# Two transformer blocks on one core: when the adaLN products run, and which engine computes silu and the convolution's first tap

## The chip, the cores and the metric

The kernel runs on one core of one Trainium2 chip. The metric is the device time of one execution in microseconds (us), as the median of several runs. Five engines work in parallel, each on a queue of its own that it takes strictly in order: TensorE (PE, matmuls, with PEld for its weight loads), VectorE (DVE), ScalarE (ACT), GpSimd (POOL) and SyncE (SP, which issues most of the transfers here). An instruction starts when the one before it on its engine is done with and the semaphores that it waits for have come.

## What is computed

Two blocks of a transformer on 256 tokens with 1024 channels, in fp32. The first has an in-projection, a mixer of three branches (a gated linear recurrence "LRU", gated linear attention "GLA", and block attention "MoBA"), an out-projection and a SwiGLU FFN, with RMS norms. The second is a two-layer model whose norms are modulated by a condition vector c (adaLN): a short convolution with its FFN, then attention with forget gates ("FoX") with its FFN. Cut to what matters here:

```python
f = (silu(h @ w_ffn_gate) * (h @ w_ffn_up)) @ w_ffn_down      # all three FFNs have this form

shift, scale, gate, ... = split(silu(c) @ w_ada + b_ada)      # adaLN, and the same with w_ada_kv
h = x * (1 + scale) + shift

gb, gc, v = split(h @ w_in, 3)                                # short convolution
u = gc * v
y = (gb * (w0 * u[t-2] + w1 * u[t-1] + w2 * u[t])) @ w_out

k, v = h @ w_k, h @ w_v
log_f = log_sigmoid(h @ w_f + b_f)                            # forget gates
F = cumsum(log_f)
logits[t, s] = q[t] . k[s] / sqrt(d) + F[t] - F[s]            # s <= t
```

## The kernel before

Activations lie transposed, channels on the 128 partitions and the 256 tokens along the free axis, so 1024 channels are 8 tiles of 128x256. All weights come as 128x128 blocks in the order of use, eight to a tile `raw` of 128x1024 fp32 (512 KB, four buffers, issued by SP, L125). `weights` splits each tile: ACT rounds it to `wh` (L142), DVE subtracts to `wl` = raw − wh (L148), each with five buffers. A block's product is three matmuls, `wh` with the rounded activation, `wl` with it, and `wh` with the activation's rest (L160 to L162 in `mm3`, L195 to L201 in `ksteps`). Over the kernel there are 296 such tiles.

The adaLN products silu(c) @ w_ada are not matmuls. They are 112 calls of `gemv` (L360 on): SP loads a 512 KB tile `gw` (L366, three buffers), and DVE multiplies it by the broadcast silu(c), `cact`, and accumulates into one column of `ada` (L369). Where they stand in the program is set by a rate: each single product of a stage adds `grate` to an account, each pair twice that, and `fill` calls `gemv` whenever the account reaches one. `GR` holds the rates, for the first FFN, its down-projection with the norm, the convolution, the second block's first half (out-projection `co`, FFN), its down-projection, the keys, values and attention, and the last FFN. `ada_cols` (L387) makes all products that its columns still lack. `silu_c` (L470) loads c and computes `cact`.

The stages run in the order: in-projection and mixer; the out-projection of the first block (`partial("out")`, one k step per finished head pair, and `post_rms`); FFN 0; its down-projection `d0` with a norm; the convolution (first eight products in one `kouter`, then one by one; c_c L1200 on ACT, c_up L1203 and c_y L1205 to L1208 on DVE, then the split yh, yl); its out-projection `co` with a norm; FFN 1, whose first products are begun before the norm is known (`lazy`, finished by lz_c, ff_g, ff_u L1042 to L1049); `d1`; wk, wv and the forget gates (`fox_gates`, L813 to L835, with the logarithm and exponential at L825 and L826); FoX attention (fG enters the logits at L766); wo; FFN 2; `d2`.

A scheduler of the framework sets the order of each engine's queue from the program's order and its own simulated timeline. `after`, `pipeline` and `unbroken` pin some pairs (a gw behind the wl tile issued last, `self.anchor`). The silu of the FFNs is two instructions, `silu2` (L508): tanh(x/2) on ACT (L511, `silu_t`) and (t + 1) x on DVE (L513, `silu_o`), which is twice the silu. The factor 0.5 is put into the next product: in `ffn` either the row R2h, half of the norm's row R2, scales `ff_u` (L898), or the instruction of `ff_m` has it (L905).

Of the kernel before, what the change touches and what calls it, by code (L numbers as in the profile page):

```python
# [17 lines left out]
P = 128  # L18
D = 1024
T = 256  # L20
# [8 lines left out]
LN_EPS = 1e-5  # L29
GR = (0.55, 1.2, 0.35, 0.8, 1.0, 0.8, 0.3)  # L30
QF = 1
# [32 lines left out]
class Net:  # L64
# [443 lines left out]
    def silu2(self, src):  # L508
# [5 lines left out]
        return o  # L514

    def lru(self, xin, gin, R):
        nc = self.nc
# [368 lines left out]

    def ffn(self, l, X, R=None, R2=None, first=(), rows=None):

# [4 lines left out]
        def evac(g, u):  # L893
            if R is not None:
                g2 = self.tmp("ff_g")
                V.tensor_tensor(g2, g, R, ALU.mult)
                u2 = self.tmp("ff_u")
                V.tensor_tensor(u2, u, R2, ALU.mult)  # L898
                s = self.silu2(g2)
                m = self.tmp("ff_m")  # L900
                V.tensor_tensor(m, s, u2, ALU.mult)
            else:
                s = self.silu2(g)
                m = self.tmp("ff_m")
                V.scalar_tensor_tensor(m, s, 0.5, u, op0=ALU.mult, op1=ALU.mult)  # L905
            h = self.tl(self.fp, [P, T + 2], "mh", F32R)[:, 0:T]
# [158 lines left out]
    def run(self):  # L1065
# [34 lines left out]
        go = self.pair("in_go", 0, "in_go", 1, X)  # L1100
        mix[2], mix[3] = self.gla(qk, go, la, gv, R, rc)
        mvp = self.tokmajor("in_mv", 0, 4, X)
        mv = [[], []]
# [11 lines left out]
        for i in range(4):  # L1115
# [6 lines left out]
            V.tensor_tensor(k, ps[:, 1, :], R, ALU.mult)  # L1122
            Ls = [self.attn_p(q, k, hh, self.moba_head_bias(2 * i + hh)) for hh in range(2)]
            if i:
                step(Y, i - 1)
# [5 lines left out]
        for k in range(5, NK):  # L1131
            step(Y, k)
        X = Y
        self.close()


        fg, rp, head = self.post_rms("out", X, NK, "post_mix_norm", pre)
        x1, X, steps = [], ([], []), []
# [21 lines left out]
        A.activation(R, rp, AF.Copy)  # L1160
        Rh = self.tl(self.fp, [P, T], "R2h", bufs=1)
        A.activation(Rh, rp, AF.Copy, scale=0.5)
        self.silu_c()
        self.grate = GR[0]
        self.strict = STRICT[1]
        M = self.ffn(0, X, R, Rh)
        self.grate = GR[1]
# [27 lines left out]
        for i in range(NK):  # L1195
# [8 lines left out]
            y = self.tmp("c_y")  # L1204
            V.tensor_scalar(y, up[:, 0:T], self.vec("conv_w_2", i), None, ALU.mult)  # L1205
            for j in range(1, 3):
# [256 lines left out]
```

## Time and profile before

| | us |
|---|---|
| median of three runs | 1003.15 |
| lowest and highest | 1002.32, 1003.19 |
| the profiled execution | 1002.28 |
| its span in the trace | 1000.5 |
| mean granted TensorE clock | 0.973 of full speed |
| PE busy | 936.8 (94%) |
| DVE busy | 805.7 (81%) |
| ACT busy | 528.7 (53%) |

The span is what the trace covers, from the first instruction to the last. Busy time is what instructions took, waits left out. Matmuls overlap each other, so a single one reads longer in a list (0.28 us) than the distance between two; how many fit in a window tells PE's pace. The view of PE's waits lists which instruction PE waited for, by tile and line. Lists by line give the mean duration of one instruction in ns. Timelines give start and duration, and in brackets how long the engine had been idle before and what released it.

### The profile page before, as it was taken

Reading aid. Unit: us, or ns where it says so; the run is one execution under the profiler, and the core shown is the slowest. Engines: PE = TensorE matmul, PEld = TensorE weight load, DVE = VectorE, ACT = ScalarE, POOL = GpSimd, SP = SyncE. Lnnn points to the kernel's source line nnn. Section 1 sums busy time; section 2 is a strip of 40 time slices with the busy share of each in tenths; the row PEclk is TensorE's granted clock in tenths of the full one; section 3 lists DMA queues with packets and bytes.
Section 4 is the critical chain, followed back from the end, with each engine's and each line's share of the span. In section 5 each row is a group of like instructions: output and inputs, shape, how many; then the busy total and the mean of one; then the engine's idle time right before and its main releaser. Section 6 shows DMA issues by size and latency. Waiting matters only on the chain.

```text
span 1000.5 us, 19149 instructions
## 1 busy us (share of the span) xinstructions
PE 936.8 (94%) x7442; PEld 902.4 (90%) x7442; DVE 805.7 (81%) x1578; ACT 528.7 (53%) x941; POOL 20.2 (2%) x66
## 2 busy tenths in 40 slices
PE   7989988999999879999799999999899988999996
PEld 7879887999999879998699999997788888999995
DVE  8886578999997697779999989799665898866553
ACT  7574564445443444458354444487465675545431
POOL 1211000000000000000000000000000000000001
PEclk9999998999999999999899999999899999999998
DMA  8853237888899486744999989745542366556531
GB/s 304 269 174 104 85 112 269 278 294 283 285 361 379 145 296 205 230 148 151 309 302 337 342 322 340 276 149 182 197 148 64 107 206 218 187 189 190 184 112 43
DMA packets 62346, 219.56 MB, mean 219 GB/s; under 512 B 7112, under 2 KB 8784, under 8 KB 62256
## 3 DMA queue, kind: packets, MB, share of 16 engines
q1 hardware_dynamic: 61056, 215.06, 63.5%
q0 software_dynamic: 1056, 3.16, 1.1%
q8 instruction: 58, 0.95, 0.4%
q14 instruction: 32, 0.26, 0.1%
q10 hardware_dynamic: 144, 0.13, 0.0%
HBM read 217.26 MB, written 2.63 MB: 220 GB/s over the span
## 4 chain that ended last, share of the span: by engine, by line
PE 74%; DVE 16%; issue 3%; ACT 3%; DMA 3%; SPq 0%; DVEq 0%; ACTq 0%
PE acc L160 20%; PE acc L162 20%; PE acc L161 19%; DVE wl L148 5%; DMA raw<-wts 3%; PE acc L195 3%; PE acc L196 2%; PE acc L201 2%; DVE gw L369 1%; ACT wh L142 1%; DVE ln_w L1060 1%; PE ms L807 1%; DVE yl L265 1%; DVE fg L1057 1%; PE lg L760 1%
## 5 line engine op out<-in xcount | busy, mean ns | idle before, releaser
L148 DVE TENSOR_TENSOR wl<-raw,wh 128x1024 fp32r<-128x1024 f32 (+2 forms) x296 | 355.0, 1205 | 100.9 <-ACT wh L142 99.0
L142 ACT ACTIVATE wh<-raw 128x1024 fp32r<-128x1024 f32 (+2 forms) x296 | 308.0, 1047 | 240.4 <-PE acc L162 129.3
L160 PE MATMUL acc<-yh,wh 128*128 128x256 f32 x608 | 171.1, 282 | 3.4 <-DVE ff_m L905 3.4
L160 PE MATMUL acc<-xh,wh 128*128 128x256 f32 x576 | 165.6, 287 | 7.9 <-ACT c_c L1200 3.4
L162 PE MATMUL acc<-yl,wh 128*128 128x256 f32 x608 | 171.2, 282 | 0.0
L161 PE MATMUL acc<-yh,wl 128*128 128x256 f32 x608 | 170.6, 281 | 0.0
L162 PE MATMUL acc<-xl,wh 128*128 128x256 f32 x576 | 164.2, 285 | 0.0
L161 PE MATMUL acc<-xh,wl 128*128 128x256 f32 x576 | 164.1, 285 | 0.0
L161 PE MATMUL acc<-mh,wl 128*128 128x256 f32 x528 | 148.3, 281 | 0.0
L160 PE MATMUL acc<-mh,wh 128*128 128x256 f32 x528 | 148.3, 281 | 0.0
L162 PE MATMUL acc<-ml,wh 128*128 128x256 f32 x528 | 147.7, 281 | 0.0
L369 DVE SCALAR_TENSOR_TENSOR gw<-gw,cact 128x1024 f32<-128x1024 f32 x112 | 134.6, 1217 | 0.0
L160 PEld LDWEIGHTS acc<-xh,wh 128*128 128x128 f32 x576 | 111.5, 194 | 9.8 <-ACT c_c L1200 3.6
L160 PEld LDWEIGHTS acc<-yh,wh 128*128 128x128 f32 x608 | 115.2, 190 | 3.7 <-DVE ff_m L905 3.6
L161 PEld LDWEIGHTS acc<-yh,wl 128*128 128x128 f32 x608 | 115.3, 190 | 0.4 <-issue 0.4
L162 PEld LDWEIGHTS acc<-yl,wh 128*128 128x128 f32 x608 | 114.8, 189 | 0.6 <-issue 0.6
L161 PEld LDWEIGHTS acc<-xh,wl 128*128 128x128 f32 x576 | 111.7, 194 | 0.4 <-issue 0.3
L162 PEld LDWEIGHTS acc<-xl,wh 128*128 128x128 f32 x576 | 111.1, 193 | 0.0
L161 PEld LDWEIGHTS acc<-mh,wl 128*128 128x128 f32 x528 | 99.4, 188 | 0.0
L160 PEld LDWEIGHTS acc<-mh,wh 128*128 128x128 f32 x528 | 99.3, 188 | 0.0
L162 PEld LDWEIGHTS acc<-ml,wh 128*128 128x128 f32 x528 | 99.3, 189 | 0.0
L195 PE MATMUL acc<-xh,wh 128*128 128x256 f32 (+1 forms) x256 | 67.2, 293 | 9.1 <-ACT wh L142 5.6
(407 smaller groups left out, 1553.9 us busy)
## 6 DMA issues: line engine op xcount, KB each, us to landing
raw<-wts SPq DMA_DIRECT2D x288, 512.0 KB, 4.4
gw<-ada SPq DMA_DIRECT2D x112, 512.0 KB, 5.5
raw<-wts SPq DMA_DIRECT2D x6, 256.0 KB, 5.7
m_scr<-m_row POOLq DMA_DIRECT2D x2, 768.0 KB, 5.4
ax<-xT SPq DMA_DIRECT2D x4, 256.0 KB, 4.5
m_b<-m_scr POOLq DMA_DIRECT2D x8, 128.0 KB, 4.4
out<-fg SPq DMA_DIRECT2D x8, 128.0 KB, 1.8
cst<-cst SPq DMA_DIRECT2D x1, 588.5 KB, 7.1
```

Source lines behind the costliest of these rows:

```text
L142: i = nc.scalar.activation(self.wh[:, d], r, AF.Copy)
L148: self.anchor = nc.vector.tensor_tensor(self.wl[:, d], r, self.wh[:, d].bitcast(F32), ALU.subtract)
L160: m = [mm(ps, wh, xh, start=start, stop=False), mm(ps, wl, xh, start=False, stop=False), mm(ps, wh, xl, start=False, stop=stop)]
L161: mm(ps, wl, xh, start=False, stop=False),
L162: mm(ps, wh, xl, start=False, stop=stop)]
L195: m.append(mm(outs[i], wh, X[0][k], start=k == 0 and i % per == 0, stop=False))
L196: m.append(mm(outs[i], wl, X[0][k], start=False, stop=False))
L201: m.append(mm(outs[i], wh, X[1][k], start=False, stop=False))
L265: self.lo = self.nc.vector.tensor_tensor(l, src, h.bitcast(F32), ALU.subtract)
L369: i = nc.vector.scalar_tensor_tensor(t, t, 1.0, self.cact, op0=ALU.mult, op1=ALU.mult, accum_out=self.ada[:, g:g + 1])
L760: mm(lg[hh][:, o:o + w], q[r, t], k[r, 0:w], start=o == 0, stop=False)
L807: mm(pv[64 * hh:64 * hh + 64, o:T], v[tt][vo[hh] // T][:, vo[hh] % T:vo[hh] % T + 64], pts[hh][:, p], start=tt == 0, stop=tt == 1)
```

## The change

`GR` gets other rates (0 in the convolution, lower in the second block's first half, twice as high from the keys on), and `PRE` adds calls of `gemv` in the mixer: two for each head pair, one for each late step of the out-projection, and rate 2 in its norm. `silu_c` is called in the mixer. `silu` is one ACT instruction with the function Silu, so that `silu_o` and the factors 0.5 are left out, R2h with them. The convolution's first tap c_y is an ACT copy with a scale by partition.

```diff
--- before.py
+++ after.py
@@ -27,7 +27,8 @@
 ALPHA = 4.0 ** 0.25
 RMS_EPS = 1e-6
 LN_EPS = 1e-5
-GR = (0.55, 1.2, 0.35, 0.8, 1.0, 0.8, 0.3)
+GR = (0.6, 1.15, 0.0, 0.45, 1.1, 1.6, 0.25)
+PRE = (2, 1, 2)
 QF = 1
 EV = (4, 6, 3)
 LZ = (18, 27, 30)
@@ -512,6 +513,11 @@
         o = self.tmp("silu_o")
         self.nc.vector.scalar_tensor_tensor(o, t, 1.0, src, op0=ALU.add, op1=ALU.mult)
         return o
+
+    def silu(self, src):
+        t = self.tmp("silu_t")
+        self.nc.scalar.activation(t, src, AF.Silu)
+        return t
 
     def lru(self, xin, gin, R):
         nc = self.nc
@@ -884,7 +890,7 @@
         self.warm(WARM[1], rc[:, 0:1].broadcast_to([P, T]))
         return fg, rows, head
 
-    def ffn(self, l, X, R=None, R2=None, first=(), rows=None):
+    def ffn(self, l, X, R=None, first=(), rows=None):
 
         nc = self.nc
         V = nc.vector
@@ -895,14 +901,14 @@
                 g2 = self.tmp("ff_g")
                 V.tensor_tensor(g2, g, R, ALU.mult)
                 u2 = self.tmp("ff_u")
-                V.tensor_tensor(u2, u, R2, ALU.mult)
-                s = self.silu2(g2)
+                V.tensor_tensor(u2, u, R, ALU.mult)
+                s = self.silu(g2)
                 m = self.tmp("ff_m")
                 V.tensor_tensor(m, s, u2, ALU.mult)
             else:
-                s = self.silu2(g)
+                s = self.silu(g)
                 m = self.tmp("ff_m")
-                V.scalar_tensor_tensor(m, s, 0.5, u, op0=ALU.mult, op1=ALU.mult)
+                V.tensor_tensor(m, s, u, ALU.mult)
             h = self.tl(self.fp, [P, T + 2], "mh", F32R)[:, 0:T]
             lo = self.tl(self.fp, [P, T + 2], "ml", F32R)[:, 0:T]
             nc.scalar.activation(h, m, AF.Copy)
@@ -1099,6 +1105,7 @@
         gv = self.tokmajor("in_gv", 0, 2, X)
         go = self.pair("in_go", 0, "in_go", 1, X)
         mix[2], mix[3] = self.gla(qk, go, la, gv, R, rc)
+        self.silu_c()
         mvp = self.tokmajor("in_mv", 0, 4, X)
         mv = [[], []]
         for tt in range(2):
@@ -1121,6 +1128,7 @@
             k = self.tmp("a_k")
             V.tensor_tensor(k, ps[:, 1, :], R, ALU.mult)
             Ls = [self.attn_p(q, k, hh, self.moba_head_bias(2 * i + hh)) for hh in range(2)]
+            self.gemv(PRE[0])
             if i:
                 step(Y, i - 1)
                 head(i - 1, self.attn_out(i - 1, prev, mv))
@@ -1130,10 +1138,12 @@
         head(3, self.attn_out(3, prev, mv))
         for k in range(5, NK):
             step(Y, k)
+            self.gemv(PRE[1])
         X = Y
         self.close()
 
 
+        self.grate = PRE[2]
         fg, rp, head = self.post_rms("out", X, NK, "post_mix_norm", pre)
         x1, X, steps = [], ([], []), []
         sacc = self.tmp("sacc")
@@ -1158,12 +1168,9 @@
         self.fp = self.open("ffn0", NFF)
         R = self.tl(self.fp, [P, T], "R2", bufs=1)
         A.activation(R, rp, AF.Copy)
-        Rh = self.tl(self.fp, [P, T], "R2h", bufs=1)
-        A.activation(Rh, rp, AF.Copy, scale=0.5)
-        self.silu_c()
         self.grate = GR[0]
         self.strict = STRICT[1]
-        M = self.ffn(0, X, R, Rh)
+        M = self.ffn(0, X, R)
         self.grate = GR[1]
         fg, rp, head = self.post_rms("d0", M, NFF, "post_ffn_norm")
         self.close()
@@ -1202,7 +1209,7 @@
             G.memset(up[:, 0:2], 0.0)
             V.tensor_tensor(up[:, 2:], got[("ci_v", i)], c, ALU.mult)
             y = self.tmp("c_y")
-            V.tensor_scalar(y, up[:, 0:T], self.vec("conv_w_2", i), None, ALU.mult)
+            A.activation(y, up[:, 0:T], AF.Copy, scale=self.vec("conv_w_2", i))
             for j in range(1, 3):
                 V.scalar_tensor_tensor(y, up[:, j:j + T], self.vec("conv_w_2", 8 * j + i), y, op0=ALU.mult, op1=ALU.add)
             V.tensor_tensor(y, y, got[("ci_b", i)], ALU.mult)
```

The lines of the changed file stand one further up to the new function and six or seven further behind it: wl is L149, gw L370, a_q L1127, g_kc L655, c_up L1210, fG L839. The total of `gw` by stage, counted in the two orders of DVE: mixer with its out-projection 0, then 13; FFN 0 with 19, then 21; d0 23, 22; convolution 9, 0; FFN 1 30, 17; d1 17, 18; keys and values 1, 4; gates and attention 6, 11; FFN 2 7, 6. ACT has seven table loads before and ten in the change: one more for Silu in FFN 0 and one in FFN 2, and one that reloads the exponential's table at the forget gates.

DVE in the mixer, before, between the splits of two weight tiles and the first keys of GLA (l_ names are the LRU's, g_ and ls_ the GLA's, a_ the block attention's):

```order
L544 RECIPROCAL l_e_102_515<-l_e_102_515 128x256
L561 SCALAR_TENSOR_TENSOR l_e_107_533<-l_e_107_533,l_xc_521 128x256
L544 RECIPROCAL l_e_106_529<-l_e_106_529 128x256
L505 SCALAR_TENSOR_TENSOR g_z_474<-g_z_474,ls_l_483 128x258
L148 TENSOR_TENSOR wl_1058<-raw_1055,wh_1057 128x1024
L599 TENSOR_SCALAR nsp_93_489<-g_z_474 128x2
L600 TENSOR_SCALAR sp_94_490<-g_z_474 128x2
L602 TENSOR_SCALAR g_z_474<-g_z_474 128x256
L148 TENSOR_TENSOR wl_1128<-raw_1125,wh_1127 128x1024
L619 SCALAR_TENSOR_TENSOR g_cum_711<-resetm_166,g_z_474 128x256
L632 TENSOR_TENSOR ff_u_723<-g_cum_711 128x256
```

The same place in the change:

```order
L370 SCALAR_TENSOR_TENSOR gw_1137,ada_175<-gw_1137,cact_843 128x1024
L550 RECIPROCAL l_e_106_529<-l_e_106_529 128x256
L505 TENSOR_TENSOR ls_l_483<-ls_l_483,ls_a_477 128x258
L370 SCALAR_TENSOR_TENSOR gw_1140,ada_175<-gw_1140,cact_843 128x1024
L149 TENSOR_TENSOR wl_1146<-raw_1143,wh_1145 128x1024
L149 TENSOR_TENSOR wl_1198<-raw_1195,wh_1197 128x1024
L506 SCALAR_TENSOR_TENSOR g_z_474<-g_z_474,ls_l_483 128x258
L1127 SCALAR_TENSOR_TENSOR a_q_992<-acc_931,m_R_380 128x256
L1129 TENSOR_TENSOR a_k_994<-acc_931,m_R_380 128x256
L149 TENSOR_TENSOR wl_1228<-raw_1225,wh_1227 128x1024
L370 SCALAR_TENSOR_TENSOR gw_1281,ada_175<-gw_1281,cact_843 128x1024
L370 SCALAR_TENSOR_TENSOR gw_1284,ada_175<-gw_1284,cact_843 128x1024
```

Four products `gw` stand between the wl tiles here, and four more within the 30 rows around; a_q and a_k of the first head pair stand ahead of the GLA's scan, behind which they stood.

DVE at the convolution's start, before (c_up is the first product that frees a PSUM bank there):

```order
L369 SCALAR_TENSOR_TENSOR gw_4466,ada_175<-gw_4466,cact_1828 128x1024
L369 SCALAR_TENSOR_TENSOR gw_4559,ada_175<-gw_4559,cact_1828 128x1024
L369 SCALAR_TENSOR_TENSOR gw_4622,ada_175<-gw_4622,cact_1828 128x1024
L148 TENSOR_TENSOR wl_4717<-raw_4714,wh_4716 128x1024
L148 TENSOR_TENSOR wl_4765<-raw_4762,wh_4764 128x1024
L148 TENSOR_TENSOR wl_4796<-raw_4793,wh_4795 128x1024
L148 TENSOR_TENSOR wl_4827<-raw_4824,wh_4826 128x1024
L1203 TENSOR_TENSOR c_up_4687<-acc_4432,c_c_4685 128x256
L369 SCALAR_TENSOR_TENSOR gw_4744,ada_175<-gw_4744,cact_1828 128x1024
L369 SCALAR_TENSOR_TENSOR gw_4854,ada_175<-gw_4854,cact_1828 128x1024
L1205 TENSOR_SCALAR c_y_4690<-c_up_4687,vec_90 128x256
L148 TENSOR_TENSOR wl_4875<-raw_4872,wh_4874 128x1024
```

The same place in the change:

```order
L938 TENSOR_TENSOR xl_4421<-md_h_4418,xh_4420 128x256
L149 TENSOR_TENSOR wl_4704<-raw_4701,wh_4703 128x1024
L149 TENSOR_TENSOR wl_4749<-raw_4746,wh_4748 128x1024
L149 TENSOR_TENSOR wl_4780<-raw_4777,wh_4779 128x1024
L149 TENSOR_TENSOR wl_4811<-raw_4808,wh_4810 128x1024
L1210 TENSOR_TENSOR c_up_4674<-acc_4428,c_c_4672 128x256
L149 TENSOR_TENSOR wl_4856<-raw_4853,wh_4855 128x1024
L1214 SCALAR_TENSOR_TENSOR c_y_4677<-c_up_4674,vec_90,c_y_4677 128x256 x2
L1215 TENSOR_TENSOR c_y_4677<-c_y_4677,acc_4429 128x256
```

The five `gw` are gone, and so is the first tap (c_y from c_up and vec alone), which ACT computes.

DVE at the forget gates, before (f_z, f_F and fG are the gates, their running sum and its bf16 parts):

```order
L148 TENSOR_TENSOR wl_9179<-raw_9176,wh_9178 128x1024
L369 SCALAR_TENSOR_TENSOR gw_9206,ada_175<-gw_9206,cact_1828 128x1024
L827 SCALAR_TENSOR_TENSOR ls_a_8646<-ls_u_8649,ls_y_8647 16x256
L148 TENSOR_TENSOR wl_9242<-raw_9239,wh_9241 128x1024
L148 TENSOR_TENSOR wl_9299<-raw_9296,wh_9298 128x1024
L369 SCALAR_TENSOR_TENSOR gw_9314,ada_175<-gw_9314,cact_1828 128x1024
L828 SCALAR_TENSOR_TENSOR f_z_8642<-f_z_8642,ls_a_8646 16x256
L148 TENSOR_TENSOR wl_9389<-raw_9386,wh_9388 128x1024
L830 SCALAR_TENSOR_TENSOR f_F_8658<-f_z_8642,ls_l_8648 16x256
L833 CAST fG_128<-f_F_8658 16x256
```

The same place in the change:

```order
L149 TENSOR_TENSOR wl_9143<-raw_9140,wh_9142 128x1024
L370 SCALAR_TENSOR_TENSOR gw_9107,ada_175<-gw_9107,cact_843 128x1024
L833 SCALAR_TENSOR_TENSOR ls_a_8535<-ls_u_8538,ls_y_8536 16x256
L149 TENSOR_TENSOR wl_9200<-raw_9197,wh_9199 128x1024
L370 SCALAR_TENSOR_TENSOR gw_9215,ada_175<-gw_9215,cact_843 128x1024
L149 TENSOR_TENSOR wl_9293<-raw_9290,wh_9292 128x1024
L370 SCALAR_TENSOR_TENSOR gw_9218,ada_175<-gw_9218,cact_843 128x1024
L834 SCALAR_TENSOR_TENSOR f_z_8531<-f_z_8531,ls_a_8535 16x256
L370 SCALAR_TENSOR_TENSOR gw_9320,ada_175<-gw_9320,cact_843 128x1024
L836 SCALAR_TENSOR_TENSOR f_F_8547<-f_z_8531,ls_l_8537 16x256
L839 CAST fG_128<-f_F_8547 16x256
```

Between the same two instructions of the gates (ls_a and f_z) there is one `gw` before and there are two in the change, and a third right behind; between the start of the stage and fG there are 5 before and 12 in the change.

## Rows read from the trace of the kernel before

**Rows 1.** The page, busy us, share of the span and instructions by engine.
```profile
PE 936.8 (94%) x7442; PEld 902.4 (90%) x7442; DVE 805.7 (81%) x1578; ACT 528.7 (53%) x941; POOL 20.2 (2%) x66
```

**Rows 2.** Windows: length; busy us (instructions) of PE, PEld, DVE, ACT, POOL; granted clock, DMA share, GB/s.
```profile
60.00:80.00 20.00, 15.09 (x100) 13.47 (x99) 19.65 (x65) 13.55 (x33) 5.04 (x10) 0.83 0.65 191
80.00:100.00 20.00, 20.00 (x169) 18.02 (x168) 11.45 (x39) 8.67 (x20) 1.06 (x2) 1.00 0.29 90
374.00:378.00 4.00, 4.00 (x19) 4.00 (x20) 4.00 (x12) 0.20 (x1) 0.20 (x2) 0.50 0.90 336
461.00:497.00 36.00, 26.43 (x181) 25.42 (x182) 36.00 (x71) 20.01 (x39) 0.00 (x0) 0.88 0.77 252
520.00:600.00 80.00, 80.00 (x682) 80.00 (x681) 72.58 (x126) 38.62 (x64) 0.00 (x0) 1.00 0.93 334
660.00:705.00 45.00, 43.94 (x266) 36.38 (x265) 43.43 (x84) 37.41 (x73) 0.00 (x0) 1.00 0.63 209
```

**Rows 3.** PE's waits, whole span: waiting <- waited for: us, times, longest.
```profile
PE lg L766 <- DVE fG L833: 4.6, 1, 4.6
...
PE acc L160 <- DVE ff_m L905: 3.4, 1, 3.4
...
PE acc L160 <- ACT c_c L1200: 3.4, 1, 3.4
...
PE ms L654 <- DVE g_kc L649: 3.3, 1, 3.3
...
PE acc L160 <- DVE c_up L1203: 2.9, 1, 2.9
...
PE acc L160 <- DVE ff_u L898: 1.6, 1, 1.6
```

**Rows 4.** PE's waits from 461 to 497 us.
```profile
PE acc L201 <- DVE yl L265: 5.3, 4, 2.5
PE acc L198 <- DVE yl L265: 2.3, 1, 2.3
PE acc L195 <- ACT lz_c L1042: 2.1, 1, 2.1
```

**Rows 5.** Groups by line: op, shapes, count | busy us, mean ns | idle before, releaser.
```profile
L369 DVE SCALAR_TENSOR_TENSOR gw<-gw,cact 128x1024 f32<-128x1024 f32 x112 | 134.6, 1217 | 0.0
...
L513 DVE SCALAR_TENSOR_TENSOR silu_o<-silu_t,acc 128x256 f32<-128x256 f32 x38 | 15.5, 414 | 10.0 <-ACT silu_t L511 10.0
```

**Rows 6.** Timeline of DVE from 45 to 76 us: start, us, instruction, [idle before].
```profile
45.37 1.23 DVE L148 TENSOR_TENSOR wl<-raw,wh 128x1024 fp32r<-128x1024 f32 x1 [0.42 <-ACT wh L142]
...
48.15 1.23 DVE L148 TENSOR_TENSOR wl<-raw,wh 128x1024 fp32r<-128x1024 f32 x1 [0.69 <-ACT wh L142]
...
52.58 0.29 DVE L543 TENSOR_SCALAR l_e<-l_e 128x256 f32<-128x256 f32 x1 [2.33 <-ACT l_e L542]
...
61.02 1.22 DVE L148 TENSOR_TENSOR wl<-raw,wh 128x1024 fp32r<-128x1024 f32 x1 [0.27 <-ACT wh L142]
...
70.01 0.89 DVE L649 COPY g_kc<-ms 64x128 f32<-64x128 f32 x3
```

**Rows 7.** Timeline of DVE from 358 to 375 us.
```profile
359.02 1.22 DVE L369 SCALAR_TENSOR_TENSOR gw<-gw,cact 128x1024 f32<-128x1024 f32 x1
...
360.17 1.22 DVE L369 SCALAR_TENSOR_TENSOR gw<-gw,cact 128x1024 f32<-128x1024 f32 x1
```

**Rows 8.** Timeline of ACT from 357 to 375 us.
```profile
369.52 1.06 ACT L142 ACTIVATE wh<-raw 128x1024 fp32r<-128x1024 f32 x1 [6.10 <-DMA raw<-wts]
```

**Rows 9.** Groups by line of DVE from 647 to 709 us.
```profile
L148 DVE TENSOR_TENSOR wl<-raw,wh 128x1024 fp32r<-128x1024 f32 x19 | 23.0, 1215 | 1.6 <-ACT wh L142 1.6
L369 DVE SCALAR_TENSOR_TENSOR gw<-gw,cact 128x1024 f32<-128x1024 f32 x5 | 6.1, 1213 | 0.0
```

**Rows 10.** Timeline of ACT from 695 to 699 us.
```profile
696.55 1.28 ACT L825 ACT_TABLE_LOAD   x1
697.85 0.42 ACT L825 ACTIVATE ls_l<-ls_u 16x256 f32<-16x256 f32 x1
```

## The prediction

> **What bounds the kernel now.** The first view is the busy line of the page: TensorE (PE) is busy for 936.8 of 1000.5 us, VectorE (DVE) for 805.7, ScalarE (ACT) for 528.7 [rows 1]. A share of the whole span hides that stages have different limits, so the second view is the table by windows [rows 2]. In the middle of the first part of the second block's FFN (520 to 600 us) PE runs without a break: 682 matmuls in 80 us, 0.117 us each, while DVE is busy for 72.58. There PE is the limit, and DVE work that is taken out is worth nothing. From 60 to 80 us (mixer), 461 to 497 (start of the second FFN) and 660 to 705 (keys, values and forget gates) DVE is busy for 19.65 of 20, 36.00 of 36 and 43.43 of 45 us, and PE makes only 100, 181 and 266 matmuls where its pace would allow 170, 307 and 384. There DVE is the limit and each microsecond on it counts. From 80 to 100 PE runs unbroken again with DVE busy for 11.45. The third view, PE's waits, names the instruction that came last [rows 3]: in the mixer g_kc (3.3); at the convolution's start c_up (2.9) and c_c (3.4); at the forget gates fG (4.6); in the last FFN ff_m (3.4); and for the second FFN's start by itself [rows 4] yl, four times in 5.3 and once 2.3, with lz_c 2.1. All but c_c and lz_c are DVE instructions.
>
> **What is priced.** A gw product takes 1.217 us [rows 5], but starts 1.15 us apart when back to back (359.02 to 360.17) [rows 7]; I use 1.15. The change moves 112 of them and alters none. So their price is where they stand: in a stretch that DVE limits 1.15 each, elsewhere none. By the program's order the saturated stretches lose 5 (convolution), 3 (second FFN's start, 8 to 5) and 1 (last FFN's start, 3 to 2), and gain 8 (mixer) and 7 (keys, values and gates, 5 to 12). The balance is six more there, +6.9 us before gaps are filled.
>
> **Mixer: +5.5 us.** Between the wl tile of 45.37 us and g_kc at 70.01 [rows 6] the new order has eight gw products, 9.2 us, where there were none. DVE was idle there before four instructions: 0.42, 0.69, 2.33 and 0.27, together 3.7 us [rows 6]. A gw needs only its transfer and the vector cact, so it can fill these: 9.2 − 3.7 = +5.5. Their order behind this point also brings the second head pair's softmax ahead of g_kc; this is the same work earlier, and PE does the matmuls of that pair before its wait in exchange, so I cost it at nothing. Bounds: +3, if half of what is left over runs while PE still has split weights; +9, if no gap is filled. The five later gw products of this stage fall where DVE has 8.55 of 20 us free [rows 2]: nothing. silu_c is issued earlier in the program, but its instructions stand at the same place of DVE's order before and after: nothing.
>
> **First FFN: −0.3.** ff_u no longer needs R2h (the halved row), so PE's wait of 1.6 for ff_u [rows 3] shortens by about one 128x256 instruction of 0.414 [rows 5]. The rest of the stage is at PE's pace: its 22 silu_o products, 0.414 each [rows 5], are covered by the matmuls, as are the two gw products that it gains. If that cover were gone, the 22 would be worth 9.1 us; the unbroken window says it is not [rows 2].
>
> **Convolution: −6.** Ahead of c_up stand three gw products (from 359.02 [rows 7]), then four wl tiles; behind c_up two more, as the order shows. Without the three, c_up comes 3.45 earlier, which removes PE's wait of 2.9 [rows 3]. Without the two, the chain c_y, yh, c_c behind it comes 2.3 earlier, of a wait of 3.4. From 374 to 378 us PE had a granted clock of 0.50, the lower of its two levels, after it had stood idle: 19 matmuls where 34 would go, 1.8 us [rows 2]; I count 0.8 of that. Sum −6.0. What is late next is the raw transfer: ACT waited 6.10 for it at 369.52 [rows 8], and SyncE's queue, which issues gw and raw transfers in order, had issued the five gw transfers of this stage in between; they are gone too. Bounds: −2.9, if only the first wait goes; −8.1 with both waits and the whole clock. The first tap moves from DVE to ACT, eight instructions in all; ACT is busy for 53% [rows 1] and the convolution's middle runs under PE, so it is worth nothing there.
>
> **Second FFN's start: −5.** Three gw products fewer (3.45) and three silu_o (1.2 at 0.414 each [rows 5]) in a stretch where DVE never idles [rows 2]: −4.6; part of the low clock after the waits goes with them, −0.4. Bounds −3.5 (gw alone) and −8 (the waits for yl, 5.3 + 2.3 [rows 4], all gone). The other 19 silu_o and ten fewer gw products of the rest of this FFN stand under a PE at its pace: nothing.
>
> **Keys, values, gates: +6.5.** Of gw products 5 stand before fG now [rows 9], by the new order 12: 7 × 1.15 = +8.05, less the DVE idle time of this stretch before wl, 1.6 [rows 9]. All of it lands on PE's wait for fG (4.6 [rows 3]), since the forget gates stand behind all of them on DVE and the attention's logits behind fG on PE. Bounds +4.5 (PE's unsplit work covers two of them) and +10 (no gap filled, and the added reload of the exponential's table, 1.28 [rows 10], late as well).
>
> **Last FFN: −2.** One gw and two silu_o fewer ahead of the ff_m on which PE waits 3.4 [rows 3]: 1.15 + 0.8. Bounds −3 and 0.
>
> **Table loads: nothing.** The change adds three on ACT. One is 1.28 us, and the activation behind it starts at its end (696.55, then 697.85) [rows 10]. ACT is 53% busy [rows 1], and two of the three come at an FFN's start, where PE waits for DVE, so I count 0; on the path they would be 3 × 1.28 = 3.85. The Trainium skill ("ScalarE: Activation LUTs", section "What ACT_TABLE_LOAD costs") puts a switch at about 2.66 us, the load of about 1283 ns and a drain of about 1380 ns. The trace agrees on the load, and shows no such drain between the load and the activation; by the page, three switches on the path would be an estimated 8.0 us.
>
> **Sum.** 5.5 − 0.3 − 6.0 − 5.0 + 6.5 − 2.0 = −1.3 us. The profiled execution took 1002.28 us in a span of 1000.5; with the change 1001.0 by its measure. It stands 0.87 below the median of the runs, 1003.15, so against the median the forecast is **1001.9 us**. That is within 0.2% (2.0 us, about what a measurement of this kernel can tell from no change): two gains at transitions are paid for at two others.
>
> **Rivals.**
> *Inserted products hide (faster).* Where the DVE work between two wl tiles is short, a gw beside each tile is free: a tile feeds 24 matmuls, 2.8 us at PE's pace, and costs DVE 1.15, as in 520 to 600, where PE never breaks [rows 2]. If half of the mixer's and of the keys' stretch is like that, their terms of 5.5 and 6.5 fall to 6.0 together and the time is 995.9. For it: the gw products are placed one or two behind a wl tile, not in a heap. Against it: DVE is busy for 19.65 of 20 and 43.43 of 45 us there. It decides once PE's wait for g_kc stays under 6.
> *Transfers held in SyncE's queue (slower).* The mixer and the keys get 15 more gw transfers of 512 KB between raw transfers, in one queue in order, into a ring of three gw buffers. A gw transfer whose buffer isn't free holds the raw transfers behind it. The price is the ACT wait that the convolution shows with its gw transfers around, 6.10 [rows 8], once: 1001.9 + 6.1 = 1008.0. For it: that row. Against it: raw buffers are four deep, and the gw products leave at DVE's turn. It decides once ACT's wait for a raw transfer before fG is longer than DVE's own queue.
> *Table loads on the path (slower).* If the three loads stand where ACT is awaited (silu_t behind ff_g, the forget gates' exponential), 3.85 more: 1005.7. By the page's figures it would be an estimated 1009.9. For it: two of the loads come right ahead of an FFN's first silu. Against it: ACT's 53%.
>
> **How the numbers follow.** The sum as forecast 0.42, with its own range of 999.4 to 1004.4, half of the doubt of its four large terms: 0.15 of it below 1001.15, 0.27 within. Hidden products 0.28, all faster. Held transfers 0.22 and loads 0.08, both slower. So faster 0.43, same 0.27, slower 0.30. The range goes from 995.5, just below the first rival, to 1008.5, just above the second; the sums of all lower and all upper bounds lie outside of it.
>
> **What would show it.** Right: PE's waits for c_up and c_c gone or under 1 us each; the waits for yl at the second FFN's start down to some 3 us in all; g_kc some 5 us later with a wait of 8 to 9; the wait for fG at 10 to 12; the windows in the FFNs unchanged at 117 ns per matmul with DVE busy less. Wrong: waits for g_kc and fG that stay as they are (then the first rival), ACT idle for raw ahead of them (the second), or PE waiting on silu_t behind a load (the third). The forecast fails as a whole if DVE turns out idle in the mixer's saturated stretch while PE waits there.

## The result: 1.4% slower, and the profile after

The changed kernel takes 1015.23 us (median of four runs, 1014.2 to 1016.9) against 1002.74 for the kernel before (four runs, 997.55 to 1003.19). The ratio of the means is 1.0138 with a 95% interval of 1.0101 to 1.0175 (that of the medians is 1.0125). The forecast was 1001.9 with a range of 995.5 to 1008.5: the time lies above the range. The profiled execution took 1016.90 us in a span of 1015.2.

The busy line of the page, changed kernel (as in [rows 1]):

```profile
PE 941.5 (93%) x7442; PEld 904.7 (89%) x7442; DVE 783.5 (77%) x1504; ACT 534.2 (53%) x951; POOL 19.6 (2%) x66
```

DVE is busy for 22 us less than in [rows 1], and the kernel is slower. PE's waits over the whole span of the changed kernel (columns as in [rows 3]):

```profile
PE lg L772 <- DVE fG L839: 11.4, 1, 11.4
...
PE ms L703 <- ACT ln_t L700: 6.2, 1, 6.2
...
PE lg L744 <- DVE a_L L735: 5.0, 2, 4.5
...
PE lg L723 <- DVE a_mx L728: 4.0, 2, 2.5
...
PE acc L202 <- DVE yl L266: 3.4, 2, 3.2
...
PE acc L196 <- ACT lz_c L1048: 3.0, 1, 3.0
...
PE acc L161 <- DVE ff_m L911: 3.0, 2, 1.5
...
PE ms L487 <- DVE yl L266: 2.1, 3, 1.4
PE acc L161 <- ACT c_c L1207: 1.7, 1, 1.7
...
PE ms L660 <- DVE g_kc L655: 0.6, 1, 0.6
```

The wait for fG has grown from 4.6 to 11.4 [rows 3]. The waits for c_up (2.9) and one half of the wait for c_c (3.4) are gone, and the wait for ff_m, 3.4 in one piece, is 3.0 in two, of which 1.5 is new at the second FFN. Three waits were not in the list of before: ln_t (6.2), a_L (5.0) and a_mx (4.0). All three are in the mixer, and g_kc, which the forecast named, is nearly gone (0.6) since PE now stops earlier, at the softmax of the head pairs that was brought ahead.

Windows of the mixer, changed kernel (columns as in [rows 2]):

```profile
60.00:80.00 20.00, 11.32 (x75) 9.69 (x74) 20.00 (x61) 10.72 (x25) 2.44 (x7) 0.75 0.88 314
80.00:100.00 20.00, 18.93 (x131) 16.63 (x131) 12.99 (x33) 7.71 (x18) 2.05 (x4) 0.82 0.27 77
100.00:120.00 20.00, 13.83 (x92) 11.29 (x93) 14.69 (x49) 7.40 (x18) 1.07 (x2) 0.78 0.64 217
```

The last of these stretches in the kernel before:

```profile
100.00:120.00 20.00, 20.00 (x153) 17.18 (x151) 12.23 (x37) 12.02 (x31) 0.00 (x0) 1.00 0.33 107
```

DVE is saturated from 60 to 80 us as before, but from 100 to 120 us, where PE ran without a break, it is now idle for 6 of 20 us while DVE is busy for only 14.69.

Where the time went can be counted: both traces have 7442 matmuls on PE, so the start of the n-th matmul of one, counted from 0, can be set against the n-th of the other (inside a stage the order differs, at the stages' borders it does not; only the border at 447 lies inside the mixer, and a few matmuls on the figure there is 0.5 higher). In us, changed less before, by stage:

```
stage (matmuls)                       forecast   measured
mixer up to PE's restart (to 447)       +5.5       +7.8
rest of the mixer (to 1038)              0         +9.9
first FFN (to 2373)                     -0.3       +0.1
norm behind its d0 (to 2646)             0         +0.8
convolution's start (to 2797)           -6.0       -6.9
second FFN's start (3420 to 3796)       -5.0       -2.7
keys, values, gates (4970 to 5392)      +6.5       +9.3
last FFN's start (6097 to 6195)         -2.0       -3.7
all (to 7363)                           -1.3      +14.6
```

The rest between these stages is within 0.2. So 9.9 of the 15.9 us by which the sum failed lie in one stretch that the forecast had put at nothing. These stages, here and below, are of one execution of each kernel: the two traces are 14.6 us apart, the medians 12.5, and executions of one kernel differ by up to 7.8 (999.85 to 1007.69 in the first kernel below), so a difference of 1 us in a stage shows little by itself.

### The profile page after: what moved, and what is told of

Read it like the earlier page. It is cut to its first block, busy times and chain, and to the rows that moved or that the text cites. A ratio compares the mean times of both kernels' runs of the same rounds, so it can differ in the third digit from the quotient of the medians.

```text
span 1015.2 us, 19113 instructions
## 1 busy us (share of the span) xinstructions
PE 941.5 (93%) x7442; PEld 904.7 (89%) x7442; DVE 783.5 (77%) x1504; ACT 534.2 (53%) x951; POOL 19.6 (2%) x66
## 4 chain that ended last, share of the span: by engine, by line
PE 77%; DVE 14%; issue 3%; DMA 3%; ACT 2%; POOL 0%; DVEq 0%; ACTq 0%; SPq 0%; POOLq 0%
PE acc L161 19%; PE acc L163 19%; PE acc L162 19%; DVE wl L149 4%; PE acc L196 3%; PE acc L197 3%; PE acc L202 3%; DVE gw L370 2%; DMA raw<-wts 1%; DMA gw<-ada 1%; ACT wh L143 1%; PE acc L252 1%; PE acc L251 1%; PE acc L250 1%; PE ms L813 1%
## 5 line engine op out<-in xcount | busy, mean ns | idle before, releaser
L149 DVE TENSOR_TENSOR wl<-raw,wh 128x1024 fp32r<-128x1024 f32 (+2 forms) x296 | 355.4, 1206 | 129.4 <-ACT wh L143 127.9
L370 DVE SCALAR_TENSOR_TENSOR gw<-gw,cact 128x1024 f32<-128x1024 f32 x112 | 134.6, 1217 | 3.3 <-DMA gw<-ada 3.2
```

What stands on the lines that cost most here:

```text
L149: self.anchor = nc.vector.tensor_tensor(self.wl[:, d], r, self.wh[:, d].bitcast(F32), ALU.subtract)
L370: i = nc.vector.scalar_tensor_tensor(t, t, 1.0, self.cact, op0=ALU.mult, op1=ALU.mult, accum_out=self.ada[:, g:g + 1])
```

## The experiments

Twelve kernels ran, each against the kernel before on the same chip, whose median was 1001.8 to 1002.6 in these comparisons. Theory A: a product costs its time wherever it stands ahead of something on which PE waits, whatever DVE's mean load there. Theory B: other parts of the change reorder the mixer. Theory C: the products' transfers hold the raw transfers. The mixer's loss below is the distance of the 1038th matmul to that of the kernel before.

**No product in the mixer** (the changed kernel with other rates):

```diff
-GR = (0.6, 1.15, 0.0, 0.45, 1.1, 1.6, 0.25)
-PRE = (2, 1, 2)
+GR = (0.93, 1.15, 0.0, 0.5, 1.1, 1.6, 0.25)
+PRE = (0, 0, 0)
```

> The changed kernel, but with no adaLN product in the mixer: PRE is (0, 0, 0), and the 13 products go to the first FFN, under matmuls (GR[0] 0.93), with one more per stage here or there. Theory A (place: each product that stands on VectorE ahead of something that PE waits for costs its time, wherever VectorE's mean load is): the mixer returns to its old course, 17.7 us less than the changed kernel, so about 997.5. Theory B (the rest of the change reorders the mixer: silu_c called there, the new table loads): no gain, about 1015. Theory C (the 13 transfers, not the products, hold the raw transfers): as A, 997.5; told apart from A by a later run.

Measured: 1002.48 us (10 runs), ratio to before 1.0008 (0.9989 to 1.0027). The mixer is back to −0.2 us, with silu_c called there and the same table loads, so theory B falls. The windows of this kernel are nearly those of the kernel before ([rows 2], and the line for 100 to 120 us above):

```profile
60.00:80.00 20.00, 15.11 (x100) 13.49 (x99) 19.66 (x65) 13.54 (x33) 5.05 (x10) 0.83 0.64 190
80.00:100.00 20.00, 20.00 (x168) 18.02 (x168) 11.47 (x39) 8.65 (x20) 1.06 (x2) 1.00 0.30 90
100.00:120.00 20.00, 20.00 (x152) 17.19 (x151) 12.21 (x37) 12.00 (x31) 0.00 (x0) 1.00 0.35 107
```

The total is 5 us above what was expected. The profiled execution (1007.69, the highest of the ten) shows where: +2.9 at the first FFN's start, +3.0 at the norm behind d0, +4.3 in the FoX attention and +1.6 ahead of the last FFN. The first and the third have their explanation below; how much of the four is in the median isn't settled.

**Only the five late products, only the pairs' eight**:

```diff
-GR = (0.6, 1.15, 0.0, 0.45, 1.1, 1.6, 0.25)
-PRE = (2, 1, 2)
+GR = (0.83, 1.15, 0.0, 0.45, 1.1, 1.6, 0.25)      # and 0.74 for the pairs alone
+PRE = (0, 1, 2)                                    # and (2, 0, 0)
```

> The changed kernel without the two products for each head pair (PRE (0, 1, 2)); the five late products of the out-projection stay, eight go to the first FFN. The traces put 7.8 us of the mixer's loss ahead of TensorE's restart and 9.9 behind it. Theory A: only the first part goes, 1015.2 - 7.8 = 1007.4, with nw_y's chain of GLA's norm still cut up by products and TensorE's wait for ln_t still near 6 us. If instead the second loss only follows from the first (the delayed start pushes GLA's norm behind the head pairs), both go: 997.5.

> The changed kernel with the two products for each head pair, without the five late ones (PRE (2, 0, 0)); five go to the first FFN. Theory A: the second part goes, 1015.2 - 9.9 = 1005.3, and TensorE's wait for ln_t with it. If the second loss follows from the first: it stays, 1015.

Measured: 1002.24 us with the late ones (ratio 1.0001, 0.9986 to 1.0016) and 1004.78 with the pairs' (1.0018, 1.0007 to 1.0028). PE's waits with the late products alone:

```profile
PE ms L703 <- ACT ln_t L700: 5.8, 1, 5.8
...
PE ms L660 <- DVE g_kc L655: 3.3, 1, 3.3
```

and with the pairs' products alone, which has no wait for ln_t:

```profile
PE lg L744 <- DVE a_L L735: 5.0, 2, 4.5
...
PE lg L723 <- DVE a_mx L728: 3.7, 2, 2.5
...
PE ms L660 <- DVE g_kc L655: 0.6, 1, 0.6
```

The late five lose 0.7 us to PE's restart and 7.1 behind it; the pairs' eight lose 7.4 to the restart and 0.5 behind it. So the two losses are separate: the second does not follow from the first. Together they lose 7.8 + 7.9 = 15.7 of the 17.7; 2.0 come only with both. The total with the late ones is 5 us below what was expected: its second FFN's start gains 4.3 and its last FFN's 4.8, more than in the changed kernel, and its keys and gates lose 7.7, less.

What the late five do is seen on DVE. GLA's norm is a chain of some ten small instructions, g_vv to nw_y, nearly each of which needs the one before. Its first and last on DVE in the kernel before:

```profile
91.96 0.17 DVE L689 TENSOR_SCALAR g_vv<-ms 128x8 f32<-128x8 f32 x1 [0.41 <-PE ms L687]
...
94.62 0.17 DVE L287 SCALAR_TENSOR_TENSOR nw_y<-nw_q,nw_y 128x8 f32<-128x8 f32 x1
```

2.8 us from start to end. In the changed kernel:

```profile
104.87 0.16 DVE L695 TENSOR_SCALAR g_vv<-ms 128x8 f32<-128x8 f32 x1
...
107.29 1.22 DVE L370 SCALAR_TENSOR_TENSOR gw<-gw,cact 128x1024 f32<-128x1024 f32 x1
...
109.34 1.23 DVE L370 SCALAR_TENSOR_TENSOR gw<-gw,cact 128x1024 f32<-128x1024 f32 x1 [0.75 <-DMA gw<-ada]
...
114.00 0.17 DVE L288 SCALAR_TENSOR_TENSOR nw_y<-nw_q,nw_y 128x8 f32<-128x8 f32 x1
```

9.3 us: two products stand inside the chain, the second of which waited 0.75 for its transfer, along with two wl tiles and head-pair work; the other three of the late five stand ahead of it. Of the 6.5 us by which the chain is longer, the two products and the wait are some 3.1. The rest is a second wl tile (1.1) and instructions of the head pairs (some 2.5), which stood outside of it before: a changed order, not the products' own time. With the late products alone four of the five stand inside a chain of 12.2 us, 4.6 of it, and one of them waits 0.90 for its transfer. PE waits for the chain's end (ln_t, 6.2), and then starts at the lower clock. Windows of the changed kernel:

```profile
100.00:110.00 10.00, 8.50 (x68) 7.83 (x67) 8.17 (x24) 4.72 (x11) 1.07 (x2) 1.00 0.72 228
110.00:120.00 10.00, 5.33 (x24) 3.46 (x26) 6.51 (x26) 2.68 (x7) 0.00 (x0) 0.55 0.56 206
```

24 matmuls in the second window, in which PE was busy for 5.33 us: at the pace of the first window (68 in 8.50) it would have made 43. Set against the kernel before, PE is 8.3 us late ahead of the wait, 14.6 behind it, and 17.7 some 30 matmuls later, where it stays: some 3 us beside the wait.

**The old rate from the keys on**:

```diff
-GR = (0.6, 1.15, 0.0, 0.45, 1.1, 1.6, 0.25)
+GR = (0.83, 1.15, 0.0, 0.45, 1.1, 0.8, 0.25)
```

> The changed kernel with the old rate 0.8 from the keys on instead of 1.6, so that 6 products stand in the keys and gates as before (5), not 13; the others go to the first FFN. Theory A: the stage's 9.1 us go but for one product, 1015.2 - 9.1 + 1.1 = 1007.2, and the wait for fG is near the 4.6 of before instead of 11.4. If the reload of the exponential's table and the logarithm's later place make that wait, it stays over 9 and the time near 1014.

Measured: 1008.41 us (ratio 1.0054, 1.0038 to 1.0071), as expected within 1.2. The stage loses 1.0 instead of 9.3, and the wait for fG is near that of before (4.6 [rows 3]):

```profile
PE lg L772 <- DVE fG L839: 5.9, 1, 5.9
```

**Products without transfers, transfers without products** (the mixer's thirteen in the changed kernel):

```diff
-            i = nc.sync.dma_start(t, self.a["ada"][g])
-            if g < 3:
-                self.after(i, self.dma)
-            i = nc.vector.scalar_tensor_tensor(t, t, 1.0, self.cact, op0=ALU.mult, op1=ALU.mult,
+            src = t
+            if g < 13:
+                src = self.cact
+            else:
+                nc.sync.dma_start(t, self.a["ada"][g])
+            i = nc.vector.scalar_tensor_tensor(t, src, 1.0, self.cact, op0=ALU.mult, op1=ALU.mult,
```

and in the other kernel, which keeps the transfers:

```diff
-            i = nc.vector.scalar_tensor_tensor(t, t, 1.0, self.cact, op0=ALU.mult, op1=ALU.mult,
+            w = 8 if g < 13 else D
+            i = nc.vector.scalar_tensor_tensor(t[:, 0:w], t[:, 0:w], 1.0, self.cact[:, 0:w], op0=ALU.mult, op1=ALU.mult,
```

Each leaves 13 columns of the adaLN result uncomputed or incomplete.

> The changed kernel; the 13 products of the mixer leave out their transfers and multiply cact by itself, so that 13 columns of the adaLN result aren't computed. VectorE has the same 13 instructions of 128x1024 at nearly the same places. Theory A (VectorE's time in front of what TensorE waits for): the mixer keeps its loss, 17 us within 3, so 1012 to 1018. Theory C (the transfers hold the raw transfers in SyncE's queue): the mixer is back within 3 us of before, so about 1000.

> The changed kernel; the 13 products of the mixer keep their transfers of 512 KB, but multiply only the first 8 of 1024 columns, so that 13 columns of the adaLN result are not complete. The scheduler then also keeps VectorE's old order in the mixer. Theory A: mixer within 2 us of before, total 1015.2 - 17 = 998. Theory C: the loss stays, 1012 or more.

Measured: 1014.66 us without the transfers (ratio 1.0136, 1.0117 to 1.0156), with a mixer loss of 18.1; 1000.31 with the transfers and short products (0.9991, 0.9977 to 1.0005), with a loss of 1.0. Windows without the transfers:

```profile
60.00:80.00 20.00, 11.57 (x73) 9.78 (x72) 20.00 (x63) 11.47 (x25) 4.09 (x10) 0.72 0.55 161
...
100.00:120.00 20.00, 14.67 (x100) 12.30 (x101) 14.25 (x46) 8.30 (x20) 1.06 (x2) 0.83 0.55 182
```

and with transfers and short products:

```profile
60.00:80.00 20.00, 15.80 (x96) 13.78 (x95) 19.65 (x73) 12.84 (x30) 4.49 (x10) 0.74 0.92 339
...
100.00:120.00 20.00, 19.72 (x147) 16.68 (x146) 12.21 (x41) 11.24 (x30) 0.00 (x0) 1.00 0.53 187
```

The DMA share from 60 to 80 us is 0.55 in the kernel that keeps the loss and 0.92 in the one that loses it. So theory C falls for the mixer: it is the products' stay on DVE. What stays open is how much of it is the time itself and how much the order that the scheduler chose around the long products; short products also bring the old order back, so this pair doesn't part the two. The one figure for it is the chain above, where 3.1 of 6.5 us are the products' own.

**Silu on ScalarE alone** (the kernel before with this part of the change, rates and tap as before):

```diff
-                s = self.silu2(g2)
+                s = self.silu(g2)
-                V.tensor_tensor(u2, u, R2, ALU.mult)
+                V.tensor_tensor(u2, u, R, ALU.mult)
```

> The kernel before with the one change that silu is one instruction on ScalarE (no silu_o, no R2h, three more table loads); all rates and the tap as before. By the terms of the forecast: -0.3 at the first FFN, -1.2 at the second FFN's start, -0.8 at the last FFN's start: -2.3, so 1000.3 against 1002.6. If the loads lie on the path: up to 3.85 more, 1004. If the stage walk of the changed kernel is right that the second FFN's start gave 2.7 and the last 3.6 with both products and silu changed, silu's own part is between -1 and -5.

Measured: 998.01 us (12 runs) against 1001.79, ratio 0.9965 (0.9954 to 0.9976). By stages: −1.3 around the first FFN's start, −0.9 at the convolution's start, −0.2 at the second FFN's, +0.7 at the gates, +1.6 ahead of the last FFN and −3.6 at its start, where the wait for ff_m, 3.4 [rows 3], is 1.5. At the gates the reload is on the path; ACT in this kernel:

```profile
691.22 1.28 ACT L828 ACT_TABLE_LOAD   x1
692.52 0.42 ACT L828 ACTIVATE ls_y<-ls_a 16x256 f32<-16x256 f32 x1
```

The load is again 1.28 us and the activation follows at its end. The wait for fG is 5.7 instead of 4.6 [rows 3], with the same five products ahead of it: one more load costs 1.1. The Trainium skill ("ScalarE: Activation LUTs", section "What ACT_TABLE_LOAD costs") puts a switch at about 2.66 us; these rows and the wait bear out the load alone.

**The convolution's products alone, the tap alone** (the kernel before):

```diff
-GR = (0.55, 1.2, 0.35, 0.8, 1.0, 0.8, 0.3)
+GR = (0.8, 1.2, 0.0, 0.8, 1.0, 0.8, 0.3)
```

```diff
-            V.tensor_scalar(y, up[:, 0:T], self.vec("conv_w_2", i), None, ALU.mult)
+            A.activation(y, up[:, 0:T], AF.Copy, scale=self.vec("conv_w_2", i))
```

> The kernel before with only the convolution's products moved: GR[2] is 0, and GR[0] 0.8, so that the nine go to the first FFN. Theory (the products ahead of c_up and the transfers ahead of raw cause the waits): the convolution's start gives the 6.9 us that the changed kernel gained there, but for the denser first FFN: 1002.2 - 6.9 = 995.3. If the tap has a part in that gain, less: e10 then shows the rest.

> The kernel before with only the convolution's first tap on ScalarE. Forecast: nothing, 1002.2 within 1. If a step between two engines lengthens the chain c_up, tap, c_y at the convolution's start: up to 1 us slower; if it is part of the 6.9 us gain: faster by up to 1.5.

Measured: 996.27 us with the products out of the convolution (ratio 0.994, 0.9927 to 0.9953) and 1002.47 with the tap moved (0.9994, 0.9984 to 1.0003). The convolution's start gains 6.7 by the first and 0.2 by the second: the gain is the products', the tap is worth nothing, as forecast. Of the first, PE's waits at the convolution's start:

```profile
PE acc L160 <- ACT c_c L1200: 1.7, 1, 1.7
PE acc L160 <- DVE c_up L1203: 0.2, 1, 0.2
```

The other side is the first FFN, whose rate is now 0.8: PE's wait for nw_y at its start is 5.2 instead of 3.2, for the same reason as in the mixer, since a product more stands in front of the chain of that norm. It loses 2.7.

**The rate of the keys alone** (the kernel before):

```diff
-GR = (0.55, 1.2, 0.35, 0.8, 1.0, 0.8, 0.3)
+GR = (0.55, 1.2, 0.35, 0.55, 1.0, 1.6, 0.3)
```

> The kernel before with only the rate from the keys on raised to 1.6 (11 products in keys and gates, not 5; the second FFN has nine fewer, three of them at its start). Theory A: six products more at 1.15 plus the low clock behind a longer wait, the keys and gates lose 7 to 8 us, the second FFN's start gains 2.5, together about 1007. If the changed kernel's 9.1 us there came in the main from the reload of the table: below 1003.

Measured: 1012.56 us (ratio 1.0101, 1.0087 to 1.0116), 5.6 above what was expected. Keys and gates lose 6.9, with a wait for fG of 10.8. The second FFN's start gains nothing (0.4 lost): its waits for yl are shorter, but a wait for ff_m of 3.0, which the kernel before has not there, takes that back. And 5.8 are lost in the FoX attention, which the expectation had not thought of. DVE there:

```profile
737.70 1.22 DVE L369 SCALAR_TENSOR_TENSOR gw<-gw,cact 128x1024 f32<-128x1024 f32 x1
...
738.85 1.22 DVE L369 SCALAR_TENSOR_TENSOR gw<-gw,cact 128x1024 f32<-128x1024 f32 x1
```

and PE behind it:

```profile
741.41 0.45 PE L792 MATMUL ms<-ident,a_L 128*128 128x128 f32 x1 [2.57 <-DVE a_L L784]
```

Two products stand ahead of a head's softmax, and PE waits for that (a_L). DVE is busy for 24.01 of 38 us in this stretch. The last FFN's start gains 3.6 with one product fewer near it and with the old silu, as much as the new silu alone gained (3.6): there the wait for ff_m, 3.4 [rows 3], fell to 1.5, here it is gone and one for yl of 1.4 is new. The two gains don't add.

**Two versions that keep the gains.** The first is the changed kernel with PRE at zero and the old rate of the keys:

```diff
-GR = (0.6, 1.15, 0.0, 0.45, 1.1, 1.6, 0.25)
-PRE = (2, 1, 2)
+GR = (0.9, 1.15, 0.0, 0.7, 1.1, 0.8, 0.35)
+PRE = (0, 0, 0)
```

> A version that keeps what paid: silu on ScalarE, the tap on ScalarE, no product in the convolution; but none in the mixer (PRE (0, 0, 0)) and the old rate in keys and gates (0.8). 32 products stand in the first FFN, 10 to 15 in the second. Theory A, from the stage differences of the changed kernel: -0.3 (first FFN) -6.9 (convolution) -2.7 (second FFN's start) -3.6 (last FFN), +1.3 (gates): -12.2, about 990.4. If the denser rate in the first FFN costs there, or its end, as in the first run without mixer products (+2.8 at its start and +3 at its end), some 996.

The second has the rate at zero up to the seventh column pair of the first two FFNs and up to the attention:

```diff
-GR = (0.6, 1.15, 0.0, 0.45, 1.1, 1.6, 0.25)
+GR = (1.1, 1.0, 0.0, 1.2, 0.9, 0.0, 0.6)
-PRE = (2, 1, 2)
+PRE = (0, 0, 0)
...
+            if l < 2 and j == n + 6:
+                self.grate = GR[3 * l]
-        self.grate = GR[0]
+        self.grate = 0
-        self.grate = GR[3]
+        self.grate = 0
-        self.grate = GR[5]
+        self.grate = 0
```

> As the version that kept the gains (993.64), and with the products also out of the starts of the two FFNs and of the keys: the rate is zero until the seventh column pair of the first and second FFN and zero in the keys, and higher behind. Two products are left at the second FFN's start (10), seven in the keys and gates as they are pinned there. Theory A: the first FFN's start gets back its 2.7 us, the second's 8 x 1.15 at most, of which PE's pace takes some half: 993.6 - 2.7 - 4 = 987. If the products of the convolution's end of list (2) or the dense rates break PE's pace in the FFNs: 993 or more.

Measured: 993.64 us (ratio 0.9925, 0.9912 to 0.9938) and 990.59 (0.988, 0.9867 to 0.9893). Both beat both kernels. The first lost 2.8 at the first FFN's start, with a wait for nw_y of 5.7. The second gets that back (3.1 better than before there), and gains 9.8 at the second FFN's start, a gain that is complete at the 3620th matmul, up to which no product is left of nine; but it loses 3.0 at the norm behind d0 and 6.5 in the FoX attention, into which products of the keys were pushed. DVE there:

```profile
721.70 1.22 DVE L370 SCALAR_TENSOR_TENSOR gw<-gw,cact 128x1024 f32<-128x1024 f32 x1
...
727.35 1.23 DVE L370 SCALAR_TENSOR_TENSOR gw<-gw,cact 128x1024 f32<-128x1024 f32 x1 [1.13 <-DMA gw<-ada]
```

PE waits 3.6 behind these for the softmax. So the expected 987 was missed, in the main by the same mechanism once more. The keys and gates show its limit: no product is left of the five ahead of fG, and the wait for it is down from 4.6 [rows 3]:

```profile
PE lg L772 <- DVE fG L839: 2.4, 1, 2.4
```

Yet the stage gains nothing (0.2 lost), since PE comes to that wait 3.0 late, with waits for yl (0.9 and 1.4) that the kernel before has not. A product that is taken out need not give its time back.

## Why the prediction was wrong, step by step

**Mixer, to the restart.** Forecast +5.5 within +3 to +9, measured +7.8. That the eight products cost DVE's time is right (alone they give 7.4), and they did fill the gaps: between its wl tile at 45.94 us and g_kc DVE is idle for 0.25 us, where it was for 3.3 [rows 6]. What was mis-sized is the head pair's softmax brought ahead, which the forecast would "cost at nothing". g_kc comes at 81.99, not at 70.01 [rows 6]:

```profile
81.99 0.88 DVE L655 COPY g_kc<-ms 64x128 f32<-64x128 f32 x3
```

From the wl tile to g_kc DVE takes 36.05 us instead of 24.64: 9.1 more for the products, 3.0 less of idle time, and 5.3 more of other work, of which 3.3 are the second head pair's. PE waits for that pair (a_mx 4.0, a_L 5.0), and not for g_kc, where the forecast had seen a wait of 8 to 9. In all it waits 9.6 up to the restart; before, it was 4.9 (g_kc 3.3 and another 1.6). What makes up the other 3.1 of the 7.8 is not shown; PE's granted clock was 0.50 from 78 to 86 us.

**Mixer, the rest.** This is the step that failed: "The five later gw products of this stage fall where DVE has 8.55 of 20 us free [rows 2]: nothing." Measured +9.9, of which the late five by themselves give 7.1. A window's free time was read as cover. But the products don't stand in the free time; they stand in the queue, in front of and inside a chain of small instructions on which PE waits, and an in-order queue makes that chain longer by each of them, and the order around it changes with them. The order of DVE showed it, since nw_q stands on both sides of a gw there; the forecast looked only at the place of the first eight.

**First FFN.** −0.3 forecast, +0.1 measured, and silu alone gave −1.3 around its start: small either way. Products under PE's pace cost nothing: behind its start this FFN shifts by 0.1 at most, in all kernels that ran.

**Convolution.** −6.0 forecast, −6.9 measured, −6.7 by the products alone, 0.2 by the tap. The sum is right and so are the products as the cause, but its parts are not all: c_up is gone, c_c fell from 3.4 to 1.7 and not to under 1. The waits give 4.6 and not 5.2; the other 2.3 fit the clock, of which the forecast counted 0.8: granted 0.88 from 358 to 386 us before, and 1.00 in the same stretch of the change, 376 to 398.

**Second FFN's start.** −5.0 forecast, −2.7 measured. The waits for yl fell from 7.6 [rows 4] to 3.4, near the forecast, but the wait for lz_c rose from 2.1 to 3.0 and a wait for ff_m of 1.5 is new. The three silu_o, forecast at 1.2, are worth 0.2 by themselves (silu alone). With nine products fewer in that stretch the last version gained 9.8, 1.1 each.

**Keys, values, gates.** +6.5 forecast within +4.5 to +10, measured +9.3: 6.8 in the wait for fG, on which all of it was to land, and 2.3 ahead of it, where a wait of 1.4 for yl is new. Seven products were priced at 8.05, less 1.6 for gaps. The gaps were not filled; DVE of the changed kernel from 656 to 728 us:

```profile
L149 DVE TENSOR_TENSOR wl<-raw,wh 128x1024 fp32r<-128x1024 f32 x19 | 22.9, 1215 | 1.2 <-ACT wh L143 1.2
L370 DVE SCALAR_TENSOR_TENSOR gw<-gw,cact 128x1024 f32<-128x1024 f32 x12 | 14.4, 1216 | 1.2 <-DMA gw<-ada 1.2
```

It is idle for 1.2 before wl, against 1.6 before [rows 9], and for 1.2 before gw, waiting for its transfer. The products alone cost 6.9 for six, and the table load, forecast at nothing, 1.1.

**Last FFN.** −2.0 forecast, −3.7 measured, more than its bound of −3. The wait for ff_m fell by 1.9, as forecast, from 3.4 to 1.5. The other part is PE's clock, which the term left out. The stretch in the kernel before:

```profile
825.00:842.00 17.00, 13.56 (x101) 13.22 (x99) 14.38 (x28) 8.86 (x17) 0.00 (x0) 0.90 0.79 264
```

and in the changed kernel, where the granted clock no longer falls behind the wait:

```profile
843.00:857.00 14.00, 12.47 (x106) 12.27 (x106) 11.61 (x22) 9.32 (x18) 0.00 (x0) 1.00 0.81 266
```

About as many matmuls took 17 us and now take 14.

**Rivals.** None was right. Hidden products: the opposite came true. Held transfers: refuted for the mixer by the kernel without transfers; at the gates, where DVE waits 1.2 for gw, no run tests them. Loads on the path: 1.1 of 3.85. The side of the result had a chance of 0.30; the mechanism that decided it had none.

## What to carry to other kernels

Work that nothing waits for is not free because its engine is half idle: on an in-order queue it costs its time wherever it stands in front of, or inside, a serial chain that another engine waits for. Before you place filler, mark these chains (norms, softmaxes, gates, the first evacuation of a stage) and keep it behind them; the stages where the waiting engine runs unbroken are where it is free. And for a kernel whose order a scheduler sets, read the new order around each such chain, not only the count by stage: where a product went in, other work moved as well.

## What the runs showed that was not expected

A product can wait for its own transfer: 0.75 us in the mixer and 1.2 (in two pieces) at the gates of the changed kernel, 1.13 in the last one, each time where several products stand close together. And after a wait PE pays again: with a granted clock of 0.55 behind the wait for ln_t it made 24 matmuls in 5.33 busy us where 43 would go, some 3 us beside the wait of 6.2, and in the last FFN the shorter wait gave back the clock as well.
